# State-space stage of a streaming encoder step: turn counts rounded inside one PSUM sum, selection rows kept as constants over 16 partitions, and the sample's input columns transposed for 16 groups at once

## The chip, the cores and the metric

The program runs on one core of a Trainium2 chip. The metric is the device time of one launch, in microseconds. The core has a matrix engine (PE in the profile, its weight loads PEld), a vector engine (DVE), an activation engine (ACT), a general engine (POOL), and a queue engine (SP) that issues most of the transfers. Each engine takes its own instructions strictly in order, and semaphores hold an instruction until what it needs is there.

## The reference

One step of a two-layer encoder trunk. Layer 0 mixes tokens with a diagonal complex state-space layer and a gated product, layer 1 with sparse attention; a convolutional feed-forward block follows each. The prompt has 1,024 tokens, the sample 32 tokens with a state carried in. Only the state-space mixer matters here:

```python
def s5_mixer(u, h0_re, h0_im, lam_re, lam_im, log_dt, b_re, b_im, c_re, c_im, d_skip, w_glu, b_glu):
    uf = u.reshape(b, t, SSM_GROUPS, SSM_GROUP)               # 64 groups of 16 channels
    a_re, a_im, bb_re, bb_im = s5_discretize(...)             # a = exp(lambda*dt), 64 states a group
    bu_re = jnp.einsum('btgc,gpc->btgp', uf, bb_re)           # and bu_im
    bu_re = bu_re.at[:, 0].add(a_re * h0r - a_im * h0i)       # the carried state enters at token 0
    _, _, h_re, h_im = lax.associative_scan(_cplx_combine, (ar, ai, bu_re, bu_im), axis=1)
    y = einsum('btgp,gcp->btgc', h_re, c_re) - einsum('btgp,gcp->btgc', h_im, c_im)
    y = y + d_skip.reshape(SSM_GROUPS, SSM_GROUP) * uf
    z = jax.nn.gelu(y.reshape(b, t, D_MODEL))
    g = z @ w_glu + b_glu
    return g[..., :D_MODEL] * jax.nn.sigmoid(g[..., D_MODEL:]), h_re[:, -1], h_im[:, -1]
```

## The kernel before

**Blocks of 8 tokens.** The scan runs over blocks of 8 tokens: 128 blocks of the prompt and 4 of the sample, plus two columns that hold states, so a row has C = 134 columns. The 64 groups are taken as 8 output tiles `o` of 8 groups, and each tile as three sub-tiles `s` of 3, 3 and 2 groups (402, 402 and 268 columns).

**What is done for a sub-tile.** `angles(o, s)` computes, for every state and block, the rotation angle in turns, its cosine and sine, and the inputs laid out by block. `states(d, w)` multiplies inputs by the input maps, rotates, scans along the blocks on DVE (`en`) and rotates back (`pp`). `outputs(d, w)` sums three products into the output rows. For each tile, `taps(o)` builds the maps' factors (`ix`, `cp`) on DVE with helper products `tt` on POOL, and `maps(o, d)` forms `kr` and `inm` from them on PE and ACT.

**Order.** The code asks for `angles` two sub-tiles ahead of `states`, and for `taps` and `maps` of the next tile during the present one. A scheduler in the building layer merges this into one order for each engine. `angles` of a sub-tile stands on PE ahead of `states` two sub-tiles earlier, so everything that `angles` waits for on PE also holds that work.

**Angles.** A selection row `sel` is built on POOL for each sub-tile (L622): a constant row of block numbers `cval`, times the column of a 64-group identity, over 128 partitions. PE multiplies it with three weight tiles `wo` (high part, rounded part, low part of the turns per block). The first product (L626) goes to a PSUM tile of its own; DVE rounds it to whole turns by adding and subtracting a large constant (`kk`, L628); PE then sums the high part (L630), minus the whole turns (L631, weights `ngi`) and the low part (L632) in a second PSUM tile. ACT makes `cs` (cosine and sine) from that. Three prompt transposes (L641) and three sample transposes of 6 columns each (L642) fill one PSUM tile `pu`, which ACT copies to `ut` (L644).

**Sample inputs.** `ssm_input` normalizes the sample rows into `us` on DVE, moves them by 8 transfers from SBUF to SBUF into rooms that are free by then (L516), and copies them to 8 tiles `um` on ACT and DVE (L519, L521). It also makes the 8 prompt tiles `u` (L507), six on DVE and two on POOL.

**The scan's first column.** In `states`, ACT writes column 0 of `ga` from the carried state (L657). `ga` has two buffers, so this copy waits until the scan `en` two sub-tiles earlier has read its buffer. The next instructions on ACT wait behind it.

Of the kernel before, what the change touches and what calls it, by code (L numbers as in the profile page):

```python
# [41 lines left out]
MAGF = 12582912.0  # L42
# [8 lines left out]
class Trunk:  # L51
# [265 lines left out]
    def ssm_params(self, pool, tmp, ld):  # L317

        nc, I = self.nc, self.I
        G, N = 64, 64  # L320
# [112 lines left out]

        wo = pool.tile([P, 3, 2, N], F32R, name="wo")
        wof = wo.bitcast(F32)
        two = lambda v: v.rearrange("g (h n) -> g h n", h=1).to_broadcast([G, 2, N])
        nc.vector.tensor_copy(wo[:G, 1], two(pt))
        nc.scalar.mul(wo[G:, 1], two(pt), 0.0)
        nc.scalar.copy(wo[:G, 0], wof[:G, 1])
        nc.vector.tensor_sub(pt, pt, wof[:G, 1, 0])  # L440
        nc.vector.tensor_add(st, st, pt)
        nc.vector.tensor_copy(wo[:G, 2], two(st))
        nc.vector.tensor_scalar_add(t3, st, -2e-5)
        nc.scalar.copy(wo[G:, 0], two(t3))
# [36 lines left out]

    def ssm_input(self, tmp, ld):

# [27 lines left out]

        room = [v[0:6, i : i + 1024].rearrange("c (j f) -> c j f", f=P) for v in ld["free"] for i in range(0, 3072, 1024)]
        for o in range(KD):
            t = self.xp.tile([6, 8, 8, 16], F32, tag="xh", name="um", bufs=KD)
            r = room[o]
            nc.sync.dma_start(r, us[:, o * P : (o + 1) * P])  # L516
            v = r.rearrange("c j (g q) -> c g j q", q=16)
            if o in (2, 4, 6):
                nc.vector.tensor_copy(t, v)  # L519
            else:  # L520
                nc.scalar.copy(t, v)  # L521
            um.append(t)
        return u, um

    def ssm(self):

        nc, I, O = self.nc, self.I, self.O
        C = 134
        with ExitStack() as ctx:
            pool = ctx.enter_context(self.tc.tile_pool(name="ssm", bufs=1, reuse_waits="tile"))  # L530
            with self.tc.tile_pool(name="ssmt", bufs=1, reuse_waits="tile") as tmp:
                ld = self.ssm_loads(tmp)
                ngi = pool.tile([P, P], F32R, name="ngi")
                nc.vector.tensor_scalar_mul(ngi, self.ident, -1.0)
                swap = pool.tile([P, P], F32, name="swap")
                nc.sync.dma_start(swap, I["c_swap"])
                cval = pool.tile([P, C], F32, name="cval")
                nc.sync.dma_start(cval, I["c_cval"].to_broadcast([P, C]))
                id2 = pool.tile([P, 64], F32, name="id2")
                nc.vector.tensor_add(id2, self.ident[:, 0:64], self.ident[:, 64:128])  # L540
                fcs = pool.tile([P, 2, 2, 64], F32, name="fcs")
                tz = [pool.tile([P, 8, P], F32, name=f"tz{i}") for i in range(2)]
                m8s = [pool.tile([P, 8, C], F32, name=f"m8{i}") for i in range(2)]
                sels = [pool.tile([P, 3 * C], F32R, name=f"sel{i}") for i in range(3)]
                for t in tz:
                    nc.gpsimd.memset(t, 0.0)
                for t in m8s:
                    nc.gpsimd.memset(t[:, :, 0:6:5], 0.0)
                par = self.ssm_params(pool, tmp, ld)
                u, um = self.ssm_input(tmp, ld)  # L550
            smt, wo = par["smt"], par["wo"].rearrange("p v h n -> p v (h n)")
            mq = self._fill(pool, "mq", [P, 1], -0.25)
# [61 lines left out]
            def angles(o, s):  # L614

                g0 = G0[s]
                ng = min(3, 8 - g0)
                W, W2 = ng * C, W3(ng)
                v3 = lambda t: t[:, :W].rearrange("p (g c) -> p g c", c=C)
                gg = slice(8 * o + g0, 8 * o + g0 + ng)  # L620
                sel = sels[s]
                nc.gpsimd.tensor_mul(  # L622
                    v3(sel), cval.rearrange("p (g c) -> p g c", g=1).to_broadcast([P, ng, C]),
                    id2[:, gg].rearrange("p (g c) -> p g c", c=1).to_broadcast([P, ng, C]))
                pa = self.ps()
                nc.tensor.matmul(pa[:, :W2], wo[:, 0], sel[:, :W2], start=True, stop=True)  # L626
                kk = wk.tile([P, 3 * C], F32R, tag="kk", name="kk", bufs=1)
                nc.vector.tensor_scalar(kk[:, :W2], pa[:, :W2], MAGF, MAGF, op0=ALU.add, op1=ALU.subtract)  # L628
                pb = self.ps()
                nc.tensor.matmul(pb[:, :W2], wo[:, 1], sel[:, :W2], start=True, stop=False)  # L630
                nc.tensor.matmul(pb[:, :W2], ngi, kk[:, :W2], start=False, stop=False)  # L631
                nc.tensor.matmul(pb[:, :W2], wo[:, 2], sel[:, :W2], start=False, stop=True)  # L632
                cs = wk.tile([P, 2, 3, C], F32, tag="cs", name="cs", bufs=3)[:, :, :ng]
                cos, sin = cs[:, 0], cs[:, 1]
                nc.scalar.activation(cos, v3(pb), AF.Abs)
                nc.scalar.activation(sin, v3(pb), AF.Abs, bias=mq)
                nc.scalar.activation(cos, cos, AF.Sin, scale=-2 * math.pi, bias=self.halfpi)
                nc.scalar.activation(sin, sin, AF.Sin, scale=sc2, bias=bi2)
                pu = self.ps()
                for g in range(ng):  # L640
                    nc.tensor.transpose(pu[:, g * C + 6 : (g + 1) * C], u[o][:, g0 + g].rearrange("p j q -> p (j q)"), self.ident)  # L641
                    nc.tensor.transpose(pu[:, g * C : g * C + 6], um[o][:, g0 + g].rearrange("p j q -> p (j q)"), self.ident[:6, :6])  # L642
                ut = wk.tile([P, 3, C], F32, tag="ut", name="ut", bufs=3)[:, :ng]
                nc.scalar.copy(ut, v3(pu))  # L644
                return dict(o=o, s=s, g0=g0, ng=ng, gg=gg, v3=v3, cs=cs, cos=cos, sin=sin, ut=ut)

            def states(d, w):
# [138 lines left out]
    def glu(self, after_block):  # L786
# [3 lines left out]
        with self.tc.tile_pool(name="glu", bufs=2, reuse_waits="tile") as gp:  # L790
# [993 lines left out]
```

## Time and profile before

| what | value |
|---|---|
| time, median of 3 runs | 2750.98 us (2748.64 to 2754.19) |
| profiled execution: its own time | 2755.65 us |
| profiled execution: span of instructions | 2753.9 us |
| mean granted TensorE clock | 0.978 of full speed |
| PE busy over the span | 2576.4 us (94%) |
| DVE busy over the span | 1584.6 us (58%) |
| ACT busy over the span | 1006.8 us (37%) |
| POOL busy over the span | 434.5 us (16%) |

The state-space stage takes the first 262 us of the span. After it the gated product, the feed-forward blocks and the attention fill the rest. In the profile, a line such as L622 is a line of the kernel before; `out<-in` are the program's names. "Idle before" is the time in which an engine waited just ahead of an instruction, with the instruction that ended the wait.

### The profile page before, as it was taken

The numbers are of one execution on the slowest core, as the hardware profiler recorded it, in microseconds if no ns is written. First come the engines' busy times: TensorE is split into PE (matmuls) and PEld (weight loads), VectorE is DVE, ScalarE is ACT, GpSimd is POOL, SyncE is SP. The second block draws the span as 40 slices with busy tenths as digits, with TensorE's granted clock in tenths as the row PEclk, the third lists the DMA queues.
The fourth block names the chain that finished last, engine by engine and source line by source line (L and its number), as shares of the span: only waits on it lengthen the run. The fifth ranks groups of instructions, "written<-read, shape, count | busy, mean of one in ns | idle before, by whom it ended". The sixth has DMA issues, their size and how long they took to land. (4 is left out here: it accounts for less than half of the span.)

```text
span 2753.9 us, 43113 instructions
## 1 busy us (share of the span) xinstructions
PE 2576.4 (94%) x17203; PEld 2464.9 (90%) x17203; DVE 1584.6 (58%) x3300; ACT 1006.8 (37%) x2054; POOL 434.5 (16%) x659
## 2 busy tenths in 40 slices
PE   2888999999999999998898789999999999999999
PEld 2777999999999999997788667779999999999998
DVE  8885235544444444467799887663654444444443
ACT  4576223222222222234466667772322222222222
POOL 5553001100000000011245342220200000000000
PEclk9999999999999999998899899999999999999999
DMA  4234330111111111110111301203111111111111
GB/s 93 54 59 87 99 110 1 47 47 47 46 47 46 47 47 47 46 29 22 47 61 55 97 15 40 52 14 84 32 47 47 47 47 46 47 47 47 46 39 64
DMA packets 226253, 140.35 MB, mean 51 GB/s; under 512 B 50293, under 2 KB 218653, under 8 KB 226053
## 3 DMA queue, kind: packets, MB, share of 16 engines
q1 hardware_dynamic: 222309, 133.91, 17.8%
q8 instruction: 135, 2.21, 0.3%
q10 hardware_dynamic: 3104, 2.59, 0.3%
q0 software_dynamic: 640, 1.12, 0.2%
q14 instruction: 65, 0.53, 0.1%
HBM read 112.68 MB, written 13.40 MB: 46 GB/s over the span
## 5 line engine op out<-in xcount | busy, mean ns | idle before, releaser
L160 PE MATMUL ps_mm<-xh,whi 128*128 128x352 f32 x2304 | 746.7, 324 | 4.9 <-ACT whi L151 4.9
L162 PE MATMUL ps_mm<-xh,wlo 128*128 128x352 f32 x2304 | 746.0, 324 | 0.0
L161 PE MATMUL ps_mm<-xl,whi 128*128 128x352 f32 x2304 | 745.0, 323 | 0.0
L160 PEld LDWEIGHTS ps_mm<-xh,whi 128*128 128x128 f32 x2304 | 434.5, 189 | 5.1 <-ACT whi L151 5.1
L161 PEld LDWEIGHTS ps_mm<-xl,whi 128*128 128x128 f32 x2304 | 434.5, 189 | 0.0
L162 PEld LDWEIGHTS ps_mm<-xh,wlo 128*128 128x128 f32 x2304 | 434.3, 188 | 0.2 <-DVE wlo L152 0.2
L152 DVE TENSOR_TENSOR wlo<-wraw,whi 128x1024 fp32r<-128x1024 f32 (+1 forms) x145 | 175.4, 1221 | 419.0 <-ACT whi L151 419.0
L151 ACT CAST whi<-wraw 128x1024 fp32r<-128x1024 f32 (+1 forms) x145 | 149.7, 1046 | 715.1 <-PE ps_mm L161 696.7
L1656 DVE TENSOR_TENSOR xt<-xt,ps_mm 128x352 f32<-128x352 f32 x528 | 269.5, 521 | 191.5 <-PE ps_mm L162 191.3
L160 PE MATMUL ps_mm<-hh,whi 128*128 128x352 f32 x1056 | 341.2, 323 | 1.5 <-DVE xt L1656 1.5
L161 PE MATMUL ps_mm<-hl,whi 128*128 128x352 f32 x1056 | 341.1, 323 | 0.0
L162 PE MATMUL ps_mm<-hh,wlo 128*128 128x352 f32 x1056 | 340.8, 323 | 0.0
L1637 POOL COPY tails<-a 128x2 f32<-128x2 f32 x44 | 39.6, 900 | 1235.6 <-ACT a L1626 1235.6
L160 PEld LDWEIGHTS ps_mm<-hh,whi 128*128 128x128 f32 x1056 | 198.5, 188 | 2.1 <-DVE xt L1656 2.1
L162 PEld LDWEIGHTS ps_mm<-hh,wlo 128*128 128x128 f32 x1056 | 198.5, 188 | 0.0
L161 PEld LDWEIGHTS ps_mm<-hl,whi 128*128 128x128 f32 x1056 | 198.4, 188 | 0.0
L840 PE MATMUL ps_mm<-whi,xh 128*128 128x256 f32 (+3 forms) x560 | 162.5, 291 | 20.8 <-ACT raw L1241 20.7
L1644 DVE TENSOR_TENSOR c<-c,ps_mm 128x352 f32<-128x352 f32 (+2 forms) x176 | 71.6, 428 | 162.5 <-PE ps_mm L162 116.0
L841 PE MATMUL ps_mm<-wlo,xh 128*128 128x256 f32 (+3 forms) x560 | 161.5, 289 | 0.0
L842 PE MATMUL ps_mm<-whi,xl 128*128 128x256 f32 (+3 forms) x560 | 161.1, 289 | 0.0
L1626 ACT COPY a<-ps_mm 128x352 f32<-128x352 f32 (+2 forms) x176 | 61.9, 378 | 246.4 <-PE ps_mm L162 246.3
L840 PEld LDWEIGHTS ps_mm<-whi,xh 128*128 128x128 f32 (+1 forms) x560 | 103.9, 186 | 24.6 <-ACT raw L1241 23.4
(425 smaller groups left out, 4537.7 us busy)
## 6 DMA issues: line engine op xcount, KB each, us to landing
wraw<-in_ffn_w_up_dram SPq DMA_DIRECT2D x88, 512.0 KB
wraw<-in_ffn_w_down_dram SPq DMA_DIRECT2D x44, 512.0 KB
wraw<-in_attn_w_in_dram SPq DMA_DIRECT2D x14, 512.0 KB
graw<-in_ssm_w_glu_dram SPq DMA_DIRECT2D x104, 64.0 KB
xcm<-in_x_prompt_dram SPq DMA_DIRECT2D x8, 512.0 KB
cps<-cp SPq DMA_DIRECT2D x16, 256.0 KB
xcol<-in_x_prompt_dram SPq DMA_DIRECT2D x8, 512.0 KB
qr<-qd SPq DMA_DIRECT2D x32, 128.0 KB
```

Of the source, the lines that this page charges most:

```text
L151: nc.scalar.copy(hi, raw)
L152: nc.vector.tensor_sub(lo, raw, hi.bitcast(F32))
L160: nc.tensor.matmul(ps, wh, xh, start=(i == 0), stop=False)
L161: nc.tensor.matmul(ps, wh, xl, start=False, stop=False)
L162: nc.tensor.matmul(ps, wl, xh, start=False, stop=(i == n - 1))
L840: self.nc.tensor.matmul(ps, xh, hi[:, c, a:b], start=(k == 0), stop=False)
L841: self.nc.tensor.matmul(ps, xh, lo[:, c, a:b], start=False, stop=False)
L842: self.nc.tensor.matmul(ps, xl, hi[:, c, a:b], start=False, stop=(k == KD - 1))
L1626: nc.scalar.copy(u["a"][:, co + 2 : co + 2 + n], ps[:, to - b * BLK : to - b * BLK + n])
L1637: nc.gpsimd.tensor_copy(tails[:, u["f"], 0:2], u["a"][:, TP : TP + 2])
L1644: nc.vector.tensor_mul(h, h, bv[:, to - b * BLK : to - b * BLK + n])
L1656: nc.vector.tensor_add(self.xt[:, m, blocks[b]], self.xt[:, m, blocks[b]], ps[:, :BLK])
```

## The change

Four edits, all in the state-space stage; in all later stages the order of instructions on every engine is the same as before.

1. The turns are rounded in PSUM. One PSUM tile takes five products in a row: plus the large constant (a row of ones times `big`), minus the high part, minus the constant, plus the rounded part, plus the low part. The PSUM tile of the first product, `kk` on DVE and `ngi` are gone.
2. `sel` is a constant from the host over 16 partitions, loaded once and cast once; the weights `wo` are cut into 8 tiles `wog` of 16 partitions by 16 small transfers on POOL's queue.
3. The sample's columns go through DRAM: one transfer out (`usd`), 24 transfers back into a tile of 96 partitions, four transposes and one ACT copy to `uT`. The 64 small transposes are gone; POOL copies 6 columns a group from `uT` into `ut`.
4. The copy of column 0 of `ga` stands on POOL, not on ACT.

```diff
-    def ssm_input(self, tmp, ld):
+    def ssm_input(self, tmp, ld, uT, wo):
...
-        room = [v[0:6, i : i + 1024].rearrange("c (j f) -> c j f", f=P) for v in ld["free"] for i in range(0, 3072, 1024)]
+        with self.tc.tile_pool(name="usd", bufs=1, space=bass.MemoryType.DRAM) as dp:
+            usd = dp.tile([n, D], F32, name="usd")
+            nc.sync.dma_start(usd, us)
+            um = tmp.tile([96, 4, 8, 16], F32, name="um")
+            v = usd.rearrange("(c j) (t g q) -> c t g j q", j=8, t=4, q=16)
+            for c in range(6):
+                for t in range(4):
+                    nc.sync.dma_start(um[16 * c : 16 * c + 16, t], v[c, t])
+        ps = self.ps("aux")
+        for t in range(4):
+            nc.tensor.transpose(ps[:, 96 * t : 96 * t + 96], um[:, t].rearrange("p j q -> p (j q)"), self.ident[:96, :96])
+        nc.scalar.copy(uT, ps[:, :384].rearrange("p (t c g) -> p t c g", c=6, g=16))
+
+        ws = []
         for o in range(KD):
-            t = self.xp.tile([6, 8, 8, 16], F32, tag="xh", name="um", bufs=KD)
-            r = room[o]
-            nc.sync.dma_start(r, us[:, o * P : (o + 1) * P])
...
+            t = self.xp.tile([16, 3, P], F32R, tag="xh", name="wog", bufs=KD)
+            for h in range(2):
+                nc.gpsimd.dma_start(t[8 * h : 8 * h + 8], wo[64 * h + 8 * o : 64 * h + 8 * o + 8])
+            ws.append(t)
+        return u, ws
...
+                sel = pool.tile([16, 3, 3 * C], F32R, name="sel")
+                sraw = tmp.tile([16, 3, 3 * C], F32, name="sraw")
+                nc.scalar.dma_start(sraw, I["c_sel"])
+                nc.scalar.copy(sel, sraw)
...
-                nc.gpsimd.tensor_mul(
-                    v3(sel), cval.rearrange("p (g c) -> p g c", g=1).to_broadcast([P, ng, C]),
-                    id2[:, gg].rearrange("p (g c) -> p g c", c=1).to_broadcast([P, ng, C]))
-                pa = self.ps()
-                nc.tensor.matmul(pa[:, :W2], wo[:, 0], sel[:, :W2], start=True, stop=True)
-                kk = wk.tile([P, 3 * C], F32R, tag="kk", name="kk", bufs=1)
-                nc.vector.tensor_scalar(kk[:, :W2], pa[:, :W2], MAGF, MAGF, op0=ALU.add, op1=ALU.subtract)
+                w, st = wo[o], sel[:, s, :W2]
+
                 pb = self.ps()
-                nc.tensor.matmul(pb[:, :W2], wo[:, 1], sel[:, :W2], start=True, stop=False)
-                nc.tensor.matmul(pb[:, :W2], ngi, kk[:, :W2], start=False, stop=False)
-                nc.tensor.matmul(pb[:, :W2], wo[:, 2], sel[:, :W2], start=False, stop=True)
+                nc.tensor.matmul(pb[:, :W2], big[0:1, 0], ones[0:1, :W2], start=True, stop=False)
+                nc.tensor.matmul(pb[:, :W2], w[:, 0], st, start=False, stop=False)
+                nc.tensor.matmul(pb[:, :W2], big[0:1, 1], ones[0:1, :W2], start=False, stop=False)
+                nc.tensor.matmul(pb[:, :W2], w[:, 1], st, start=False, stop=False)
+                nc.tensor.matmul(pb[:, :W2], w[:, 2], st, start=False, stop=True)
...
-                    nc.tensor.transpose(pu[:, g * C + 6 : (g + 1) * C], u[o][:, g0 + g].rearrange("p j q -> p (j q)"), self.ident)
-                    nc.tensor.transpose(pu[:, g * C : g * C + 6], um[o][:, g0 + g].rearrange("p j q -> p (j q)"), self.ident[:6, :6])
+                    nc.tensor.transpose(pu[:, g * P : (g + 1) * P], u[o][:, g0 + g].rearrange("p j q -> p (j q)"), self.ident)
                 ut = wk.tile([P, 3, C], F32, tag="ut", name="ut", bufs=3)[:, :ng]
-                nc.scalar.copy(ut, v3(pu))
+                a = o % 2 * 8 + g0
+                nc.gpsimd.tensor_copy(ut[:, :, 0:6], uT[:, o // 2, :, a : a + ng].rearrange("p c g -> p g c"))
+                nc.scalar.copy(ut[:, :, 6:], pu[:, : ng * P].rearrange("p (g c) -> p g c", c=P))
...
-                nc.scalar.copy(ga[:, :, 0], smt[:, 33, w["gg"]])
+                nc.gpsimd.tensor_copy(ga[:, :, 0], smt[:, 33, w["gg"]])
...
-            gp.tile([P, 2 * P + 64], F32, name="pad", bufs=1)
+            gp.tile([P, 2 * P - 24], F32, name="pad", bufs=1)
```

The first place is POOL at the start of the stage, from the first prompt tile `u` that POOL makes. Before, it reads (numbers tell tiles of one name apart):

```order
L507 TENSOR_TENSOR u_491<-xcm_97,rsx_443 128x8x8x16
L622 TENSOR_TENSOR sel0_128<-cval_119,id2_121 128x402
L622 TENSOR_TENSOR sel1_129<-cval_119,id2_121 128x402
L622 TENSOR_TENSOR sel2_130<-cval_119,id2_121 128x268
L507 TENSOR_TENSOR u_497<-xcm_103,rsx_443 128x8x8x16
L569 TENSOR_TENSOR tt_538<-smt_279,bsw_352 128x1024
L593 TENSOR_TENSOR dgi_554<-ident_61,dg_439 16x128
```

Now 16 transfers stand there in place of three `sel` products, 13 of them between the second `u` and the first `tt`:

```order
L507 TENSOR_TENSOR u_490<-xcm_97,rsx_442 128x8x8x16
L529 DMA wog_538<-wo_336 8x384 x2
L529 DMA wog_541<-wo_336 8x384
L507 TENSOR_TENSOR u_496<-xcm_103,rsx_442 128x8x8x16
L529 DMA wog_541<-wo_336 8x384
L529 DMA wog_544<-wo_336 8x384 x2
L529 DMA wog_547<-wo_336 8x384 x2
L529 DMA wog_550<-wo_336 8x384 x2
L529 DMA wog_553<-wo_336 8x384 x2
L529 DMA wog_556<-wo_336 8x384 x2
L529 DMA wog_559<-wo_336 8x384 x2
L581 TENSOR_TENSOR tt_575<-smt_278,bsw_351 128x1024
```

Behind the last row come `dgi`, three copies to `ut`, two copies to `ga`, two clears of `pp`, and only then the second `tt` of the tile.

The second place is PE in the middle of the stage, `angles` of a sub-tile of two groups (L608 belongs to `maps`, L653 and L654 to `states`). Before:

```order
L626 MATMUL ps_mm<-sel_130,wo 128x268
L630 MATMUL ps_mm<-sel_130,wo 128x268
L641 MATMUL ps_mm<-ident,u 128x128
L642 MATMUL ps_mm<-ident,um 128x6
L641 MATMUL ps_mm<-ident,u 128x128
L608 MATMUL ps_aux<-ident,ix 128x128 x4
L631 MATMUL ps_mm<-kk,ngi 128x268
L632 MATMUL ps_mm<-sel_130,wo 128x268
L642 MATMUL ps_mm<-ident,um 128x6
L653 MATMUL ps_mm<-ut,inm 128x134 x2
```

Now the five products of the sum stand together, and no product of the group waits for DVE:

```order
L636 MATMUL ps_mm<-ones,big 128x268
L637 MATMUL ps_mm<-sel,wog 128x268
L638 MATMUL ps_mm<-ones,big 128x268
L639 MATMUL ps_mm<-sel,wog 128x268
L640 MATMUL ps_mm<-sel,wog 128x268
L649 MATMUL ps_mm<-ident,u 128x128 x2
L662 MATMUL ps_mm<-ut,inm 128x134 x2
```

The third place is ACT where the copies of `kr` stand that `maps` of the next tile needs. Before, a copy to `ga` stands ahead of them:

```order
L637 ACTIVATE cs<-cs,halfpi 128x402
L638 ACTIVATE cs<-cs,bi_531,sc_530 128x402
L657 COPY ga<-smt 128x3
L600 COPY kr<-ps_aux 16x512 x2
L644 COPY ut<-ps_mm 128x402
```

Now it is gone, and `kr` follows the sine at once:

```order
L645 ACTIVATE cs<-cs,halfpi 128x402
L646 ACTIVATE cs<-cs,bi_566,sc_565 128x402
L612 COPY kr<-ps_aux 16x512 x2
L653 COPY ut<-ps_mm 128x3x128
L693 COPY yo<-ps_mm 128x402
```

## Rows read from the trace of the kernel before

**Rows 1.** Busy time of each engine in two stretches, granted clock at the end.

```profile
149.00:176.00 27.00, 22.18 (x130) 18.68 (x128) 20.64 (x25) 19.10 (x38) 12.55 (x15) 0.81 0.30 57
123.00:223.00 100.00, 83.86 (x529) 70.78 (x528) 79.55 (x93) 69.71 (x139) 53.91 (x68) 0.88 0.34 65
```

The columns are the stretch, its length, busy us (instructions) of PE, PEld, DVE, ACT and POOL, PE's clock, the DMA share and GB/s.

**Rows 2.** Timeline of DVE: first rotation of tile 0 and of tile 7.

```profile
81.67 0.56 DVE L659 TENSOR_TENSOR ga<-ps_mm,cs 128x399 f32<-128x399 f32 x1
...
243.39 0.57 DVE L659 TENSOR_TENSOR ga<-ps_mm,cs 128x399 f32<-128x399 f32 x1 [0.25 <-PE ps_mm L653]
```

The columns are start, duration, engine, line and operation; in brackets the idle time before and what ended it.

**Rows 3.** Timeline of PE: first products and transposes of one `angles` call.

```profile
101.55 0.43 PE L626 MATMUL ps_mm<-sel,wo 128*128 128x402 f32 x1
101.81 0.34 PE L630 MATMUL ps_mm<-sel,wo 128*128 128x402 f32 x1
102.00 0.27 PE L641 MATMUL ps_mm<-ident,u 128*128 128x128 f32 x1
102.20 0.22 PE L642 MATMUL ps_mm<-ident,um 6*128 6x6 f32 x1
102.35 0.33 PE L641 MATMUL ps_mm<-ident,u 128*128 128x128 f32 x1
```

**Rows 4.** Waits of PE in 76 to 262 us: total, times, longest.

```profile
PE ps_aux L608 <- ACT kr L600: 9.3, 5, 4.1
...
PE ps_mm L631 <- DVE kk L628: 3.2, 5, 1.3
```

**Rows 5.** Timeline of DVE, ACT and PE around two waits for `kr`.

```profile
159.21 2.63 DVE L663 TENSOR_TENSOR_SCAN en<-m,ga 128x402 f32<-128x402 f32 x1
...
161.88 0.20 ACT L657 COPY ga<-smt 128x3 f32<-128x3 f32 x1 [3.13 <-DVE en L663]
161.88 1.00 DVE L667 TENSOR_TENSOR pp<-en,cs 128x804 f32<-128x804 f32 x1
162.19 1.05 ACT L600 COPY kr<-ps_aux 16x512 f32<-16x512 f32 x2
...
162.82 1.97 PE L608 MATMUL ps_aux<-ident,ix 128*128 128x128 f32 x8 [4.07 <-ACT kr L600]
...
211.63 1.13 PE L608 MATMUL ps_aux<-ident,ix 128*128 128x128 f32 x8 [3.29 <-ACT kr L600]
```

**Rows 6.** Groups by line and shape, 55 to 262 us: the wide rounding.

```profile
L628 DVE TENSOR_SCALAR kk<-ps_mm 128x402 fp32r<-128x402 f32 x16 | 9.0, 565 | 2.6 <-PE ps_mm L626 2.6
```

The columns are busy us, mean ns of one, and the idle time before them.

**Rows 7.** Timeline of the start, and of eight transfers on POOL's queue.

```profile
44.50 9.39 POOL L507 TENSOR_TENSOR u<-xcm,rsx 128x1024 f32<-128x1024 f32 x1 [4.00 <-DVE rsx L174]
...
45.36 2.64 SPq L516 DMA_DIRECT2D bb<-us  x3
...
48.07 1.04 ACT L521 COPY um<-bb 6x1024 f32<-6x1024 f32 x1 [4.07 <-DMA bb<-us]
...
52.06 2.37 DVE L519 COPY um<-bb 6x1024 f32<-6x1024 f32 x1
...
58.38 2.02 POOL L569 TENSOR_TENSOR tt<-smt,bsw 128x1024 f32<-128x1024 f32 x1
...
62.61 1.20 DVE L576 TENSOR_TENSOR cp<-smt,ca 128x1024 f32<-128x1024 f32 x1
...
68.92 1.86 DVE L577 TENSOR_TENSOR cp<-cp,tt 128x1024 f32<-128x1024 f32 x1 [2.35 <-POOL tt L574]
...
75.59 5.14 SPq L603 DMA_DIRECT2D tz<-kr  x8
...
213.07 4.36 POOL L748 DMA_DIRECT2D g<-in_ssm_w_glu_dram  x8
```

**Rows 8.** Timeline of POOL: multiplier rows and copies of 8 and 12 elements.

```profile
219.39 1.75 POOL L583 TENSOR_SCALAR m<-smt 128x32 f32<-128x32 f32 x2 [1.96 <-DVE en L663]
221.09 0.19 POOL L669 COPY fcs<-pp 128x8 f32<-128x8 f32 x1
...
228.10 1.13 POOL L669 COPY fcs<-pp 128x12 f32<-128x12 f32 x1 [2.28 <-DVE pp L667]
```

More of the change, by code (lines that the diff above doesn't have):

```diff
@@ L432, in ssm_params @@
         nc.vector.scalar_tensor_tensor(st, raf, kb, st, op0=ALU.mult, op1=ALU.add)
-        wo = pool.tile([P, 3, 2, N], F32R, name="wo")
+        wo = tmp.tile([P, 3, 2, N], F32R, name="wo")
         wof = wo.bitcast(F32)
@@ L438, in ssm_params @@
         nc.scalar.mul(wo[G:, 1], two(pt), 0.0)
-        nc.scalar.copy(wo[:G, 0], wof[:G, 1])
+        nc.scalar.mul(wo[:G, 0], wof[:G, 1], -1.0)
         nc.vector.tensor_sub(pt, pt, wof[:G, 1, 0])
@@ L532, in ssm @@
                 ld = self.ssm_loads(tmp)
-                ngi = pool.tile([P, P], F32R, name="ngi")
-                nc.vector.tensor_scalar_mul(ngi, self.ident, -1.0)
+                big = pool.tile([16, 2, P], F32R, name="big")
+                for i, v in enumerate((MAGF, -MAGF)):
+                    nc.vector.tensor_scalar(big[:, i], self.ident[:16], 0.0, v, op0=ALU.mult, op1=ALU.add)
                 swap = pool.tile([P, P], F32, name="swap")
                 nc.sync.dma_start(swap, I["c_swap"])
[L537 to L540, printed above, removed]
                 fcs = pool.tile([P, 2, 2, 64], F32, name="fcs")
@@ L543, in ssm @@
                 m8s = [pool.tile([P, 8, C], F32, name=f"m8{i}") for i in range(2)]
-                sels = [pool.tile([P, 3 * C], F32R, name=f"sel{i}") for i in range(3)]
+                sel = pool.tile([16, 3, 3 * C], F32R, name="sel")
+                sraw = tmp.tile([16, 3, 3 * C], F32, name="sraw")
+                nc.scalar.dma_start(sraw, I["c_sel"])
+                nc.scalar.copy(sel, sraw)
+                uT = pool.tile([P, 4, 6, 16], F32, name="uT")
                 for t in tz:
@@ L549, in ssm @@
                 par = self.ssm_params(pool, tmp, ld)
-                u, um = self.ssm_input(tmp, ld)
-            smt, wo = par["smt"], par["wo"].rearrange("p v h n -> p v (h n)")
+                u, wo = self.ssm_input(tmp, ld, uT, par["wo"].rearrange("p v h n -> p v (h n)"))
+            smt = par["smt"]
             mq = self._fill(pool, "mq", [P, 1], -0.25)
@@ L557, in ssm @@
             wk = ctx.enter_context(self.tc.tile_pool(name="ssmw", bufs=1, reuse_waits="tile"))
+            ones = wk.tile([16, 3 * C], F32R, tag="kk", name="ones", bufs=1)
+            nc.vector.tensor_scalar(ones, self.ident[:16, 0:1].to_broadcast([16, 3 * C]), 0.0, 1.0, op0=ALU.mult, op1=ALU.add)
             G0 = (0, 3, 6)
@@ L1734, in host_constants @@
     ident = np.eye(P, dtype=f)
-    cval = np.concatenate([np.arange(5), [0], np.arange(128)]).astype(f)[None]
+    cval = np.concatenate([np.arange(5), [0], np.arange(128)]).astype(f)
+    sel = np.zeros((2, 8, 3, 3, 134), f)
+    for g in range(8):
+        sel[:, g, g // 3, g % 3] = cval
     inv = np.array([0x3F800000, 0x3E4693AF, 0x3D1A08C8, 0x3BEEF74E, 0x3AB95D22, 0x398FC8F8, 0x385F10C4, 0x372D07A7], np.uint32).view(f)
@@ L1745, in host_constants @@
         "c_swap": np.roll(ident, 64, axis=0),
-        "c_cval": cval,
+        "c_sel": sel.reshape(16, 3, 402),
     }
```

10 lines of the change are left out of this document (1 added, 9 removed).

## The prediction

> **What bounds the kernel now.** I read the page's busy times first: PE is busy for 94% of the span. All later stages hang on PE and keep their order, so a shift at the end of the state-space stage (262 us) should arrive at the end of the run unchanged. Only that stage is left to price. Next I read the windows in it. From 123 to 223 us PE is busy for 83.9 of 100 us and DVE for 79.6; PE's granted clock is 0.88, and in 149 to 176 us it is 0.81 [rows 1]. So PE is not full here, and its clock drops. The timeline of DVE gives the period of a tile: the first rotation of tile 0 starts at 81.67, that of tile 7 at 243.39 us [rows 2], 161.7 us for seven tiles, 23.1 us each. DVE's share of that is 0.796 x 23.1 = 18.4 us. The stage is thus bound neither by PE nor by DVE alone but by a loop of waits between engines; the list of PE's waits names the links. The largest are `kr` from ACT (9.3 us in 5 waits, longest 4.1) and `kk` from DVE (3.2 us in 5) [rows 4].
>
> The last look is at the start, where everything up to tile 0 is a chain of its own [rows 7].
>
> **Part one: the steady tiles.**
>
> *PE rows.* Per sub-tile group one 6x6 transpose goes. Its step to the next row is 0.15 us (102.20 to 102.35) [rows 3]; 56 of the 64 lie in tiles 1 to 7, so 8.4 us. The wide products: before, the first of a run takes a step of 0.26 us and the next 0.19 [rows 3], and the four stood in two runs, so 2 x 0.45 = 0.90 us. Now five stand in one run: 0.26 + 4 x 0.19 = 1.02. That costs 0.12 x 21 sub-tiles = 2.5 us. I assume that a product over 16 or 1 rows of the contraction takes as long as one over 128, since its step is set by its columns; no row shows it for these. Net 6 us less on PE.
>
> *The round trip for the turns.* `kk` goes, and with it 3.2 us of PE's waits [rows 4] and 565 ns of DVE each for 16 wide ones [rows 6], with the narrow ones about 1.34 us of DVE for a tile. A PSUM tile per sub-tile is also freed.
>
> *The `ga` copy ahead of `kr`.* This is the clearest cause in the trace. At 161.88 ACT begins the `ga` copy after 3.13 us without work, when `en` ends; `kr` follows at 162.19, and PE, which waited 4.07 us, goes on at 162.82 [rows 5]. Without the copy `kr` could start when ACT ran dry, at 158.75, 3.4 us earlier. PE's clock was at 0.81 in the stretch around it [rows 1]: over 27 us that is 27 x 0.19 = 5.1 us of full-speed work lost, part of which a PE without this hole keeps. But PE does not gain all: DVE's `pp` still ends at 162.88 [rows 5], and the outputs need it. I take 6 us for this wait with its clock, 5 us for the one of 3.29 us at 211.63 [rows 5], and 1 us for the rest, 12 in all.
>
> The sum of these is 6 + 3 + 12 = 21 us for seven tiles. I give a third of it back. DVE's own work, 18.4 − 1.3 = 17.0 us a tile, is a floor at 7 x 6.1 = 43 us of gain and does not forbid it; but when the `kr` wait goes, `pp` and `cp` of DVE are late next, and they don't move with this edit. So **−14 us**. Bounds: −30 if the clock also stays up through the stretch of 0.81 and the waits behind `pp` go with it; +3 if every gain is taken by the next wait and the PE rows cost their 2.5.
>
> *What POOL takes over.* The copies to `ut` and `ga` are small. A POOL copy of 8 elements a partition took 0.19 us, one of 12 that came while DVE worked 1.13 us [rows 8]. Two for each sub-tile are 6 x 0.2 to 6 x 1.1 = 1.2 to 6.8 us of POOL a tile, where it is busy for 54 of 100 us [rows 1]: there is room. I cost them at nothing. Their cover is the distance to `states` two sub-tiles on; if that goes, rival four comes true.
>
> [...]
>
> **Part two: the start.** Two chains meet at `maps` of tile 0.
>
> *POOL's chain.* POOL's first `u` is held from 44.50 to 53.89 while DVE makes its six, and came through when DVE's `um` copy began (52.06) [rows 7]. That copy is gone: DVE goes straight on to two products of 1.20 us (`ix`, `cp`), so I let `u` end at about 57. Then 3 transfers at 4.36/8 = 0.545 us [rows 7] to 58.6, the second `u` (as `tt`, the same shape, 2.0) to 60.6, 13 transfers (7.1) to 67.7, and `tt` (2.02) to 69.7; before, `tt` ended at 60.40 [rows 7]. DVE then adds (1.2) and multiplies (1.2); POOL's eight small rows (0.2 each) end at about 73.6, the second `tt` at 75.6, and the addition to `cp` at 76.8. Before, it ended at 70.78 [rows 7]: 6 us later. Some of that comes back, because the taps of tile 1, which before were spread between these, now follow each other. I put the first rotation of tile 0 at 85.5 in place of 81.67: **+4 us**.
>
> *SP's chain.* The transfer out starts at 45.36 and lands after about 2.7 us (the three before it were issued at 45.36, and ACT's copy began at 48.07 when the first was there [rows 7]), so by 48 to 49.5. 24 transfers at 5.14/8 = 0.64 us [rows 7] are 15.4 us, to 64 or 65; with a landing at 66 to 67 the transposes, the copy to `uT` and three `angles` calls stand before `states`. At the lower clock these are 8 to 9 us: about 75, just under POOL's chain. PE takes the four transposes in order, so its first `angles` waits for the last of the 24 transfers; before, PE's first products waited for `sel` instead.
>
> Bounds for the start: 0 if POOL gets its `u` in two or three us earlier and tile 1's taps absorb the rest; +9 if the 24 transfers take 0.72 to 0.88 us each (1.9 to 5.8 us more) and everything behind them moves.
>
> Before the change no row shows a POOL transfer while DVE is busy. [...]
>
> **The sum.** −14 + 4 = −10 us. Against the profiled run's own 2755.65 us this is 2745.6; that run stands 4.67 us above the median of the three (2750.98), so the median should be **2741 us**, a change of −0.36%. About 0.2% (5.5 us) is what a measurement of this kernel can tell from no change.
>
> **The rivals.**
>
> *One, the next wait takes it.* When `kr` comes early, `pp` and `cp` set the period, and only the 6 us of PE rows count. For it: DVE at 79.6% and every link behind it on DVE. Against it: at 161.88 the wait hung on the copy, not on `pp`. −6 + 4 = −2: **2749**, no change to be told.
>
> *Two, POOL's transfers at the start are held by DVE.* 16 transfers at up to 1.13 instead of 0.545 us are 16 x 0.58 = 9 us; but DVE has only about 5 us of ready work there before it needs `tt` itself, so +5: start +9, net −5, **2746**, also within 0.2%. The mechanism is that of POOL's `u` at 44.50 [rows 7].
>
> *Three, everything is given.* All 21 us of the steady part, and PE's clock stays up where it read 0.81 (another 5.1 us): −26 + 2 = −24, **2727**. For it: the holes of 3 to 4 us stand just where the clock is low. Against it: the waits for `pp` stay.
>
> *Four, slower: POOL becomes late.* The copies to `ut` and `ga` now stand in POOL's order between the multiplier rows `m` and `fcs`, which wait for `en` and `pp` of DVE [rows 8]. A sub-tile has 23.1 / 3 = 7.7 us; the scan itself takes 2.63 [rows 5], so 5.1 us lie between the end of one and the start of the next, for which `ga` must be there. POOL needs 1.75 us for `m` and, if `fcs` and both copies are held as at 228.10, 3 x 1.13 more: 5.1 us. That is the point from which it decides: one more held row makes each of 21 scans 1.13 us late, 23.7 us. The 21 us of part one are off it, the start's 4 on it: +7, so the median is **2758**. Against it: POOL idles for 46% of that stretch [rows 1], and its copies of 8 elements came through in 0.19.
>
> **How the numbers follow.** Chances: forecast 0.45, rival one 0.20, two 0.08, three 0.12, four 0.15. Faster by over 0.2%: forecast and three, 0.57. Within: one and two, 0.28. Slower: 0.15. The range takes one and two wholly, the nearer half of three, and the nearer half of four: 2728 to 2757. The forecast's own range, faster cases alone, is 2734 to 2745.
>
> **What would show it.** Right: no wait of PE for `kk`; `kr` on ACT with no idle time behind `en`; granted clock above 0.81 around the fourth tile; a period of about 21 us (23.1 − 14/7); the first rotation of tile 0 at 84 to 87 us. Wrong: POOL copies of over 0.5 us in most sub-tiles with PE waiting for `ut` (rival four); transfers on POOL's queue of over 0.8 us each (two); a period above 22.3 with waits for `pp` and `cp` grown (one). What would upset the whole: a stage-end shift that later stages swallow, or a wide product over 16 rows whose step is not 0.19 us.

## The result, and the profile after

The changed kernel takes 2734.84 us (median of 4 runs, 2732.57 to 2738.98) against 2751.02 us before (4 runs): a ratio of 0.994, 95% interval 0.9929 to 0.9952, or 16.2 us less. Forecast were 2741 us, a range of 2728 to 2757, and faster as the likeliest case. The profiled execution took 2738.98 us (span 2737.2), 16.7 us less than that of before.

The two stretches of [rows 1], after the change (same columns):

```profile
123.00:223.00 100.00, 88.49 (x632) 76.34 (x633) 83.65 (x101) 82.04 (x152) 63.25 (x98) 0.97 0.41 79
149.00:176.00 27.00, 23.25 (x174) 19.99 (x173) 24.50 (x29) 21.38 (x42) 17.65 (x21) 1.00 0.39 68
```

PE is busier in the same 100 us and its granted clock is 0.97, not 0.88; in the stretch that read 0.81 it is 1.00. (The same times hold other work now; over the seven tiles the clock is 0.95, and 0.91 before.) DVE's timeline gives the period, as [rows 2] did:

```profile
85.78 0.56 DVE L668 TENSOR_TENSOR ga<-ps_mm,cs 128x399 f32<-128x399 f32 x1
...
223.66 0.57 DVE L668 TENSOR_TENSOR ga<-ps_mm,cs 128x399 f32<-128x399 f32 x1 [0.25 <-PE ps_mm L662]
```

The first rotation comes 4.1 us later than before, that of tile 7 comes 19.7 us earlier: seven tiles take 137.9 us in place of 161.7, so 23.8 us are gained and 4.1 lost. Of these 19.7, 16.7 reach the end. PE's granted clock in 240 to 260 and 260 to 300 us was 1.00 twice before and is 0.91 and 0.96 now; 20 x 0.09 + 40 x 0.04 = 3.4 us, about the 3.0 that are missing. That the clock is the cause is not shown: in a second profile of the changed kernel (below) tile 7 comes 18.1 us earlier than before and the end 21.6, so what follows tile 7 differs by 6.5 us between two profiles of one kernel.

PE's waits from 76 to 262 us, in answer to [rows 4]:

```profile
PE ps_mm L691 <- DVE pp L676: 4.5, 3, 3.9
PE ps_aux L611 <- DVE cp L589: 4.1, 4, 1.9
...
PE ps_aux L131 <- DMA vrow<-in_ffn_conv_w_dram: 2.3, 1, 2.3
...
PE ps_mm L690 <- DVE ix L583: 1.6, 1, 1.6
...
PE ps_mm L691 <- POOL ga L666: 1.2, 1, 1.2
...
PE ps_aux L620 <- ACT kr L612: 0.5, 1, 0.5
```

The 9.3 us for `kr` are 0.5, the 3.2 for `kk` are gone, and the waits for `pp` and `cp`, 5.4 and 4.5 before, did not grow. Other waits did. PE now reaches the transposes of `vrow` (constants of this and later stages) at 131 us, not at 137, and stands there for 2.3 us until a transfer lands. From the first rotation of tile 0 to that of tile 7 all the waits that this view lists for PE come to 17.6 us, against 22.9 before: 5.3 less, not 12. The price on POOL is there, in the groups of POOL's instructions of the same stretch (busy us, mean ns, idle time before):

```profile
L666 POOL COPY ga<-smt 128x3 f32<-128x3 f32 x14 | 10.3, 733 | 13.0 <-DVE en L672 13.0
...
L666 POOL COPY ga<-smt 128x2 f32<-128x2 f32 x8 | 7.7, 968 | 3.0 <-DVE en L672 2.9
L652 POOL COPY ut<-uT 128x12 f32<-128x12 f32 x7 | 6.5, 931 | 10.9 <-PE ps_mm L690 10.9
...
L652 POOL COPY ut<-uT 128x18 f32<-128x18 f32 x14 | 5.3, 379 | 2.4 <-PE ps_mm L690 2.4
```

These copies took 0.4 to 1.0 us on average, not 0.2; but PE waited for them once, 1.2 us.

### The profile page after: what moved, and what is told of

Same layout as the page of the kernel before. It is cut to its first block, busy times and chain, and to the rows that moved or that the text cites. A ratio compares the mean times of both kernels' runs of the same rounds, so it can differ in the third digit from the quotient of the medians.

```text
span 2737.2 us, 43112 instructions
## 1 busy us (share of the span) xinstructions
PE 2566.2 (94%) x17167; PEld 2459.5 (90%) x17167; DVE 1560.4 (57%) x3275; ACT 1001.9 (37%) x2027; POOL 442.0 (16%) x699
## 4 chain that ended last, share of the span: by engine, by line
PE 77%; DVE 13%; ACT 4%; issue 3%; DMA 1%; POOL 1%; SPq 1%; ACTq 0%; DVEq 0%; POOLq 0%
PE ps_mm L162 19%; PE ps_mm L160 19%; PE ps_mm L161 19%; DVE junk L1169 4%; PE ps_o L1425 2%; PE ps_mm L793 2%; PE ps_mm L792 2%; PE ps_mm L791 2%; PE ps_t L1435 2%; PE ps_s L1399 1%; PE ps_s L1400 1%; ACT p L1409 1%; DVE p L1401 1%; DVE small L1182 1%; DVE score L1031 0%
```

## The experiments

"Steady" is the time from the first rotation of tile 0 to that of tile 7, from one profile each: 161.7 us before, 137.9 after. Ratios are to the kernel before on the same chip; intervals are of 95%.

**One edit alone, and one undone.** The `ga` copy moved to POOL in the kernel before:

```diff
-                nc.scalar.copy(ga[:, :, 0], smt[:, 33, w["gg"]])
+                nc.gpsimd.tensor_copy(ga[:, :, 0], smt[:, 33, w["gg"]])
```

> The kernel before with one edit: the copy of column 0 of ga stands on POOL, not on ACT. Theory L (the late kr behind that copy was the main loss): 12 us less than before, 2739 us, and PE's wait for kr falls from 9.3 us to under 2. Theory R (the gain comes from PE's rows and from the round trip for the turns; the next wait takes what the copy held): within 3 us of before, 2748 to 2751. POOL late (rival four of the prediction): slower than before.

2743.26 us, ratio 0.9965 (0.9951 to 0.9979), 9 us less; steady 153.0 us. The waits of PE say where the rest went:

```profile
PE ps_mm L631 <- DVE kk L628: 12.1, 10, 3.2
...
PE ps_aux L608 <- ACT kr L600: 1.1, 2, 0.6
```

The wait for `kr` fell from 9.3 to 1.1 us as theory L said, but `kk` rose from 3.2 to 12.1: the next wait on the same in-order engine took all of it. What gained the 9 us stands in the windows from the first rotation of tile 0 to that of tile 7, of the kernel before and of this run (columns as in [rows 1]):

```profile
81.67:243.39 161.72, 140.27 (x907) 118.52 (x907) 131.84 (x160) 108.40 (x215) 82.14 (x104) 0.91 0.33 64
```

```profile
81.89:234.90 153.01, 133.07 (x907) 111.75 (x907) 131.46 (x161) 106.04 (x195) 94.45 (x125) 0.96 0.34 68
```

PE runs the same number of rows, 907, and is busy for 7.2 us less, at a granted clock of 0.96 in place of 0.91; its idle time falls by only 1.5 us, from 21.5 to 19.9. The clock alone accounts for that: 140.27 x 0.91/0.96 = 133.0. So most of this edit's gain came as PE's clock. The opposite, the same line put back on ACT in the changed kernel:

> The changed kernel with the copy of column 0 of ga back on ACT. Theory L: the 12 us come back, 2747 us, with a wait of PE for kr of 6 to 9 us in total. Theory R: within 3 us of the changed kernel's 2735.

2754.15 us, 1.001 (1.0001 to 1.0019): 19 us slower than the changed kernel (17 against its second measurement, below) and not faster than the kernel before. Steady 153.1. Both theories were too low: the other three edits without this one bring nothing at the end of the run, though tile 7 still comes 4.7 us earlier than before. (In both runs the scheduler lets a few neighbours change places with the line.) The mechanism stands in ACT's and PE's timelines of this run:

```profile
205.97 0.20 ACT L666 COPY ga<-smt 128x3 f32<-128x3 f32 x1 [5.37 <-DVE en L672]
206.34 1.05 ACT L612 COPY kr<-ps_aux 16x512 f32<-16x512 f32 x2 [0.17 <-DMA cps<-cp]
...
206.97 1.97 PE L620 MATMUL ps_aux<-ident,ix 128*128 128x128 f32 x8 [3.31 <-ACT kr L612]
```

ACT stands 5.37 us before a copy of three elements, `kr` behind it, and PE behind `kr`; the eight transposes then take 1.97 us where the same eight took 1.13 at 160.20 in this run; PE's granted clock is 0.74 from 200 to 220 us. This is [rows 5] over again. It is not the whole loss: PE's wait for `kr` is 7.9 us in this run, that for `pp` 10.0 in place of 4.5, and over the seven tiles PE's busy time is 7.9 us longer than in the changed kernel (128.02 and 120.17 us for 853 rows each) and its idle time 7.4 us.

**The rounding alone.** In the kernel before, five products as in the diff, with `sel` still over 128 partitions:

> The kernel before with one edit: turns rounded by five products in PSUM, with the selection rows still built on POOL over 128 partitions. Theory L: 1 to 4 us less, 2747 to 2750, since 3 us of waits and 1.3 us of DVE a tile go but PE gets 2.5 us more. Theory R: 8 us less or more, 2743 or under, because DVE's relief shortens the loop. If the extra product matters more than the wait: 2752 to 2754.

2759.89 us, 1.0026 (1.0015 to 1.0036): 7.5 us slower, steady 170.2 us. Neither theory had this. PE's timeline of that run, one run of products:

```profile
230.34 0.44 PE L629 MATMUL ps_mm<-ones,big 1*128 1x402 f32 x1
230.72 0.45 PE L630 MATMUL ps_mm<-sel,wo 128*128 128x402 f32 x1
231.09 0.45 PE L631 MATMUL ps_mm<-ones,big 1*128 1x402 f32 x1
231.47 0.45 PE L632 MATMUL ps_mm<-sel,wo 128*128 128x402 f32 x1
231.76 0.35 PE L633 MATMUL ps_mm<-sel,wo 128*128 128x402 f32 x1
231.95 0.27 PE L642 MATMUL ps_mm<-ident,u 128*128 128x128 f32 x1
```

The step, from start to start, is 0.37 to 0.38 us around the products with weights of 1 row, 0.29 from the fourth to the fifth and 0.19 from there to the next row, where all have 128 rows. The granted clock is 1.00 from 228 to 233 us, so it is not the clock. A new theory (S): such a change of row count costs PE about 0.19 us. To test it, the same products with weights of 128 rows throughout:

```diff
-                big = pool.tile([16, 2, P], F32R, name="big")
-                for i, v in enumerate((MAGF, -MAGF)):
+                big = pool.tile([P, 2, P], F32R, name="big")
+                for i, v in enumerate((MAGF / P, -MAGF / P)):
...
-                nc.tensor.matmul(pb[:, :W2], big[0:1, 0], ones[0:1, :W2], start=True, stop=False)
+                nc.tensor.matmul(pb[:, :W2], big[:, 0], ones[:, :W2], start=True, stop=False)
```

> The kernel before with the rounding in PSUM alone, as in the run of that name, but the row of ones and its weights stand over 128 partitions (each weight 1/128 of the constant), so that all five products have the same number of rows. Theory S (a product costs more when the number of rows of its weights changes from the product before it: 0.38 us a step in place of 0.19): four changes in each of 24 runs go, 4 x 24 x 0.19 = 18 us less than the 2760 of that run, 2742. Rival (the run of five products itself, or what it pushes back, costs the 8 us): 2757 to 2760.

2747.06 us, 0.9985 (0.9976 to 0.9994): 12.8 us less than with one row, 5 us less than before; steady 157.1. The steps are 0.18 to 0.19 behind the first, which is 0.27:

```profile
171.48 0.43 PE L629 MATMUL ps_mm<-ones,big 128*128 128x402 f32 x1
171.75 0.34 PE L630 MATMUL ps_mm<-sel,wo 128*128 128x402 f32 x1
171.93 0.34 PE L631 MATMUL ps_mm<-ones,big 128*128 128x402 f32 x1
172.11 0.35 PE L632 MATMUL ps_mm<-sel,wo 128*128 128x402 f32 x1
```

So S holds, with 13 of its 18 us; the order of instructions on PE is the same in both runs. Over the seven tiles PE's busy time fell by 21.2 us (155.70 to 134.54) and its idle time grew by 8.0. Why PE pays for such a change is not shown by these runs, only what it pays: steps of 0.37 to 0.38 us in place of 0.18 to 0.19 for 402 columns. In the changed kernel the products stand over 1 and 16 rows and the steps between them are 0.18 to 0.19 us behind the first, so this cost isn't paid between 1 and 16 rows:

```profile
177.75 0.45 PE L636 MATMUL ps_mm<-ones,big 1*128 1x402 f32 x1
178.04 0.34 PE L637 MATMUL ps_mm<-sel,wog 16*128 16x402 f32 x1
178.23 0.34 PE L638 MATMUL ps_mm<-ones,big 1*128 1x402 f32 x1
178.42 0.34 PE L639 MATMUL ps_mm<-sel,wog 16*128 16x402 f32 x1
178.60 0.34 PE L640 MATMUL ps_mm<-sel,wog 16*128 16x402 f32 x1
178.87 0.55 PE L649 MATMUL ps_mm<-ident,u 128*128 128x128 f32 x3
179.25 0.39 PE L662 MATMUL ps_mm<-ut,inm 128*128 128x134 f32 x2
```

Edit 2 is thus what makes edit 1 cheap here; rows of ones over 128 partitions are another way. The reverse in the changed kernel, rounding on DVE again (`kk`, `ngi` over 128 rows between products over 16):

```diff
-                nc.tensor.matmul(pb[:, :W2], big[0:1, 0], ones[0:1, :W2], start=True, stop=False)
+                nc.tensor.matmul(pa[:, :W2], w[:, 0], st, start=True, stop=True)
+                kk = wk.tile([P, 3 * C], F32R, tag="kk", name="kk", bufs=1)
+                nc.vector.tensor_scalar(kk[:, :W2], pa[:, :W2], MAGF, MAGF, op0=ALU.add, op1=ALU.subtract)
+                nc.tensor.matmul(pb[:, :W2], w[:, 1], st, start=True, stop=False)
+                nc.tensor.matmul(pb[:, :W2], ngi, kk[:, :W2], start=False, stop=False)
```

> The changed kernel with the turns rounded on DVE again (kk, ngi over 128 partitions; selection rows and weights stay over 16). By the prediction's terms: 3 us of waits and 1.3 us of DVE a tile come back, 2.5 us of PE go: 2736 to 2740. Theory S adds two changes of row count in each run, 2 x 24 x 0.19 = 9 us: 2744 to 2750.

2745.65 us, 0.9977 (0.9967 to 0.9986), 8 to 11 us slower than the changed kernel; steady 150.4. As S said, and the steps between weights of 128 and of 16 rows are 0.39 and 0.37 us (at 179.10 and 179.49 in this run, granted clock 1.00). But the wait for `kk` is 10.2 us in 10 waits here, so both causes share the loss, and this run doesn't part them.

**The small transposes.** One 6x6 transpose more for each group in the changed kernel, into columns that are not read:

```diff
                     nc.tensor.transpose(pu[:, g * P : (g + 1) * P], u[o][:, g0 + g].rearrange("p j q -> p (j q)"), self.ident)
+                    nc.tensor.transpose(pu[:, 3 * P + 6 * g : 3 * P + 6 * g + 6], u[o][:6, g0 + g].rearrange("p j q -> p (j q)"), self.ident[:6, :6])
```

> The changed kernel with one 6x6 transpose more for each group (64 in all), into columns of the PSUM tile that nobody reads; it prices the 64 transposes that the change took away. If PE's rows count fully, as the prediction's first term says: 64 x 0.15 = 9.6 us more than 2735, 2744. If PE's free time covers them: under 3 us more.

2741.4 us, 0.9968 (0.9955 to 0.998), 4 to 7 us over the changed kernel's two medians; steady 148.4, 9 to 10.5 us more, in a profile whose run took 2747.01 us, 5.6 above the median. PE pays more than the prediction's 0.15 us:

```profile
186.24 0.22 PE L650 MATMUL ps_mm<-ident,u 6*128 6x6 f32 x1
186.39 0.33 PE L649 MATMUL ps_mm<-ident,u 128*128 128x128 f32 x1
186.65 0.22 PE L650 MATMUL ps_mm<-ident,u 6*128 6x6 f32 x1
186.81 0.33 PE L649 MATMUL ps_mm<-ident,u 128*128 128x128 f32 x1
```

A pair takes 0.41 to 0.42 us (186.24 to 186.65). Without the small one, three transposes take 0.38 us (178.87 to 179.25), 0.13 each. A 6x6 transpose costs 0.28 us of PE, half of it as the slower step of its neighbour: by theory S, 6 rows beside 128. Not all of it becomes time: over the seven tiles PE's busy time is 21.7 us longer than in the changed kernel, and its idle time 11.2 us shorter.

**Two edits together.** The kernel before with the `ga` copy on POOL and the rounding over 128 rows:

> The kernel before with two edits: the copy of column 0 of ga on POOL, and the rounding in PSUM with all products over 128 partitions. Alone they gave 9 and 5 us. If gains add: 2738. If one in-order wait hides the other (with the ga copy gone, PE's wait for kk grew from 3.2 to 12.1 us; with kk gone, the wait for kr stayed at 8.9): more than the sum, 2728 to 2734.

2732.77 us, 0.9931 (0.9917 to 0.9944): 20 us less than before where the parts alone give 9 and 5; steady 146.7, 15.0 less, where the parts give 8.7 and 4.7; no wait for `kr` or `kk` among PE's larger ones. That the wait for `kr` had hidden the one for `kk` is shown by the run with the `ga` copy alone, where `kk` rose; that the pair gives more than the sum is not clear of the noise of three measurements. These two edits, without edits 2 and 3, do as well as the whole change within the noise: the start is 4.6 us earlier and the steady tiles are 8.9 us longer.

**POOL's small copies.** The copy of 6 columns to `ut` on ACT:

```diff
-                nc.gpsimd.tensor_copy(ut[:, :, 0:6], uT[:, o // 2, :, a : a + ng].rearrange("p c g -> p g c"))
+                nc.scalar.copy(ut[:, :, 0:6], uT[:, o // 2, :, a : a + ng].rearrange("p c g -> p g c"))
```

> The changed kernel with the small copies to ut on ACT, not on POOL. If POOL's held copies cost anything in the steady tiles: 2 to 5 us less, 2730 to 2733. If they are covered and ACT has room: within 2 us of 2735. If a small copy ahead of kr on ACT delays kr again: 2738 to 2745.

2741.26 us, 0.9959 (0.9945 to 0.9972); steady 138.7. The interval overlaps that of the changed kernel, so no difference can be told; there is no gain, and POOL's held copies are not what limits the tiles. The time lies in the third theory's range, but its sign is missing: PE's wait for `kr` is not in the list of this run.

**The start.** The changed kernel was run again beside the last three:

> The changed kernel once more, unchanged, as the measure for the others of this call: 2733 to 2739 us by the four runs known; every theory expects the same here.

2737.59 us, 0.9945 (0.9932 to 0.9959); steady 139.5 us, so this measure moves by 1.6 us between two profiles of one kernel. The weights' transfers on ACT's queue in place of POOL's:

```diff
-                nc.gpsimd.dma_start(t[8 * h : 8 * h + 8], wo[64 * h + 8 * o : 64 * h + 8 * o + 8])
+                nc.scalar.dma_start(t.bitcast(F32)[8 * h : 8 * h + 8], wo.bitcast(F32)[64 * h + 8 * o : 64 * h + 8 * o + 8])
```

> The changed kernel with the 16 small transfers of the weights issued on ACT's queue, not on POOL's. Theory (POOL's chain sets the start): 16 x 0.52 = 8.4 us go from it, PE's three angles calls end at 67.6 and become the bound, so the first rotation comes 6 to 7 us earlier, at 79, and the time is 2728 to 2729. Rival (SP's 24 transfers set it, or DVE's taps): first rotation within 2 us of 85.8, time 2733 to 2735.

2738.39 us, 0.9955 (0.9943 to 0.9968), first rotation at 85.97: nothing gained, as the rival had it for the rotation. POOL was freed (`tt` ready at 59.94, not 68.29), but ACT's and SP's queues show another bound:

```profile
47.38 22.62 SPq L519 DMA_DIRECT2D um<-usd  x24
...
56.14 10.19 ACTq L529 DMA_DIRECT2D wog<-wo  x14
```

SP's 24 transfers took 22.62 us, where they take 11.20 in the changed kernel; PE's first transposes moved from 58.55 to 70.04. The gain on POOL's chain was lost on SP's. So POOL's chain was tested without touching a queue, by giving DVE all eight `u`:

```diff
-            (nc.gpsimd if o % 3 == 2 else nc.vector).tensor_mul(
+            nc.vector.tensor_mul(
```

> The changed kernel with all eight prompt tiles u made on DVE; POOL makes none at the start. Theory (POOL's first u, held for 11.9 us while DVE works, and the queue of transfers behind it set the start): POOL's first tt is ready 10 us or more earlier, PE's angles calls that end at 67.6 become the bound, the first rotation comes at 78 to 80 us in place of 85.8 and the time is 2728 to 2730. Rival (the transfers of the sample's columns on SP, or the taps, set it anyway): first rotation within 2 us of 85.8. Rival (POOL's 16 transfers are held in turn while DVE makes the tiles): their time grows beyond 0.8 us each and the first rotation stays after 82.

2722.25 us, 0.9886 (0.9873 to 0.99), 15 us below the changed kernel on that chip, and the fastest of all. The changed kernel's POOL against this run's:

```profile
44.07 11.94 POOL L507 TENSOR_TENSOR u<-xcm,rsx 128x1024 f32<-128x1024 f32 x1 [2.70 <-DVE rsx L174]
55.95 1.76 POOL L529 DMA_DIRECT2D wog<-wo  x3
57.73 1.91 POOL L507 TENSOR_TENSOR u<-xcm,rsx 128x1024 f32<-128x1024 f32 x1
59.57 6.67 POOL L529 DMA_DIRECT2D wog<-wo  x13
66.26 2.03 POOL L581 TENSOR_TENSOR tt<-smt,bsw 128x1024 f32<-128x1024 f32 x1
```

```profile
46.41 3.29 POOL L529 DMA_DIRECT2D wog<-wo  x6 [4.84 <-DVE u L507]
49.93 4.43 POOL L529 DMA_DIRECT2D wog<-wo  x8 [0.23 <-DVE u L507]
54.71 1.03 POOL L529 DMA_DIRECT2D wog<-wo  x2 [0.34 <-issue]
55.75 2.93 POOL L581 TENSOR_TENSOR tt<-smt,bsw 128x1024 f32<-128x1024 f32 x1
```

The first product `u` held POOL for 11.94 us with all the transfers queued behind it. Without it they go out while DVE works, at 0.55 us each, not held, and `tt` is done at 58.68, 9.6 us earlier. PE's last transposes of the three `angles` calls now run straight into `maps`, at 67.93, and the first rotation comes at 74.42, 11.4 us earlier where 6 to 8 were expected: a delay that I had left out goes too. In the changed kernel `ix` on DVE, just ahead of the first rotation, takes 3.40 us (82.46 to 85.86) beside a `tt` on POOL from 82.76; here that `tt` starts behind `ix`, which takes 1.35. At tile 7 the lead over the second profile of the changed kernel is 10.4 us, and 11.5 us at the end of these two profiles. So in these runs products of DVE and POOL that ran side by side could take far longer (`u` on POOL 11.94 us, and 1.91 with DVE idle; `ix` on DVE 3.40, and 1.35 ahead of `tt`), while POOL's transfers beside DVE's products took 0.55 us each, against 0.51 with DVE idle: rival two of the prediction, in which they are held, is not seen. Why the products took longer is not shown. Last, on top of that, the sample's columns by 6 transfers out and 6 back:

```diff
-            nc.sync.dma_start(usd, us)
+            for c in range(6):
+                nc.sync.dma_start(usd[c].rearrange("g j q -> j g q"), us[8 * c : 8 * c + 8].rearrange("j (g q) -> j g q", q=16))
...
-                for t in range(4):
-                    nc.sync.dma_start(um[16 * c : 16 * c + 16, t], v[c, t])
+                nc.sync.dma_start(um[16 * c : 16 * c + 16], usd[c].rearrange("(t g) j q -> g t j q", t=4))
```

> The run with all u on DVE, and the sample's columns by 6 transfers out and 6 back in place of 1 and 24. Theory (each small transfer costs SP about 0.47 us, and PE's first angles wait for the last): the four transposes start 4 us earlier, at 54 to 55 in place of 58.5, the first rotation at 75 to 76, the time 2724 to 2726. Rival (the longer write, in pieces of 64 bytes, takes what the shorter queue gives): no change against the run before, 2728 to 2730.

2725.75 us, 0.9902 (0.9889 to 0.9916): no gain over the run before, though the time and the rotation (76.17) are about what the theory named. PE's transposes start at 54.00 as expected, but PE then waits 2.69 us for `cp` until 65.19, and `ix` on DVE, beside POOL's `tt` again, takes 3.41 us just ahead of the first rotation. With the queue shortened, POOL's and DVE's chain of the taps is the bound; the rival's reason (64-byte pieces) was not the one: the transposes that need the last piece start 4.6 us earlier.

## Why the prediction came out, point by point

**The start, +4.** Right in its sum (+4.1 us, first rotation at 85.78 where 85.5 stood) and in its cause: POOL's chain was the later one, as PE's waits in the changed kernel show.

```profile
58.55 1.59 PE L522 MATMUL ps_aux<-ident,um 96*128 96x96 f32 x4 [16.86 <-DMA um<-usd]
...
74.80 3.57 PE L611 MATMUL ps_aux<-cp,ix 128*16 128x128 f32 x16 [7.02 <-DVE cp L589]
```

Its parts were off in both directions, and that the sum came out to 0.3 us is luck. SP's transfers took 11.20/24 = 0.47 us each, not 0.64, so that chain lay 7 us under POOL's, not just under it. On POOL the held `u` took 11.94 us to 56.0 (57 said), the 13 transfers 0.51 each, `tt` ended at 68.29 (69.7 said) and the addition to `cp` at 74.65 (76.8 said). The 2.2 us so won were lost again: from there to the first rotation it took 11.1 us, as before (10.9), not 8.7, with `ix` of 3.40 us at the end. Rival two was not put to the test in the changed kernel, where DVE had no work while the transfers went; in the run with all `u` on DVE they went beside DVE's products at 0.55 us each, where the prediction named over 0.8 as the rival's sign, so no run shows a transfer held by DVE. From the first of the four transposes to the end of the three `angles` calls PE took 9.2 us (58.55 to 67.78; 8 to 9 said). Its wide products stepped by 0.33 us there and by 0.18 to 0.19 from 82 us on, but the granted clock reads 1.00 in 58 to 68 us as in 81 to 86: no row shows the prediction's "lower clock" there as a granted clock, and the cause of the slower steps is not shown.

**The steady tiles, −14.** The direction was right, the size was not: 23.8 us. Two terms were off. "I give a third of it back" was to stand for `pp` and `cp` being late next, and their waits stayed at 4.5 and 4.1 us; what came back of the 12 us of `kr` and `kk` were other waits, `vrow` first. And the rows of PE were priced too low. The undiscounted sum was 21. Of its terms:

- PE rows, −6 net: the 6x6 transposes were priced at their own step of 0.15 us and cost 0.28 with that of the next row, so 56 are 15.7 us of PE, not 8.4. Five products take 1.12 us (177.75 to 178.87), not 1.02, since the step from 16 rows back to 128 is 0.27; the narrow ones take 0.82 (102.17 to 102.99) in place of 0.68 before. By these steps PE has some 11.5 us less to do in seven tiles, an estimate. In time the transposes are worth less: put back, all 64 cost 4 to 7 us. That five products cost so little more held only because edit 2 makes them 1 and 16 rows; my assumption that a product's step is set by its columns alone was wrong for 1 beside 128 (0.38 us for 402 columns, where products over 128 rows in a row stepped by 0.18 to 0.19).
- `kk`, −3: 5 us alone (rounding over 128 rows), and 8 to 11 when it is undone in the changed kernel, with the changes of row count that come back with it. Its relief of DVE was added up too low, 1.34 us a tile: the narrow one takes 0.43, so 2 x 0.565 + 0.43 = 1.56.
- `ga`, −12: 9 us alone and 17 to 19 when it is the last edit. It is the largest term, as said, but terms don't add in a loop of in-order waits.

**What was said to show it.** No wait for `kk`, `kr` straight behind the sine, clock at 1.00 around the fourth tile: all seen. ACT around the place of [rows 5], after the change:

```profile
156.38 0.72 ACT L646 ACTIVATE cs<-cs,bi,sc 128x402 f32<-128x402 f32 x1
157.00 1.04 ACT L612 COPY kr<-ps_aux 16x512 f32<-16x512 f32 x2
```

The period is 137.9/7 = 19.7 us, not 21. What POOL takes over was held much as in rival four's condition (0.4 to 1.0 us a copy), yet the 5.1 us of room sufficed: one wait of 1.2 us. Whether later stages swallow some of the shift can't be told: 3 of 19.7 us are missing in one profile, and in the other the end gained 3.5 us more than tile 7.

Where PE's rows are the same, its busy and idle time part the clock from the waits: most of what `ga` alone gave was clock, and put back as the last edit it cost about as much in busy as in idle time. For the whole change the rows differ too, and how the 23.8 us divide between fewer rows, clock and waits stays open.

## What to carry to other kernels

An instruction that waits on an in-order engine costs what stands behind it, and taking it away shows its worth only when the next wait of the same loop goes too (the `ga` copy: 9 us alone, 17 to 19 as the last edit): try edits in pairs and as the last one removed. Price a matmul with the row ahead of it: in these runs weights of 1, 6 or 16 rows among weights of 128 cost about two steps for one (402 columns: 0.38 us with 1 row and 0.37 to 0.39 with 16, against 0.19; a 6x6 transpose 0.28 with its neighbour's slower step, against 0.13 for one of 128), so keep small ones together. At a start-up chain, look for a long instruction that is held at the head of a queue of transfers (11.94 us here); moving those two products of POOL was worth 15 us, nearly as much as the whole change with its 16.2.

## What the hardware showed that I had not expected

- A change between weights of 1 and of 128 rows took PE's step from 0.19 to 0.38 us for 402 columns, at a granted clock of 1.00; between 1 and 16 rows it stayed at 0.18 to 0.19.
- One copy of three elements moved to another engine left PE's waits at the same total (12.5 us for `kr` and `kk` before, 13.2 after) and raised its granted clock from 0.91 to 0.96, which gave 7.2 of 8.7 us.
- 24 small transfers on SP's queue took 11.2 us beside 16 on POOL's queue (all `u` on DVE), and 22.6 us beside 16 on ACT's.
- Transfers on POOL's queue took 0.55 us each while DVE made `u` (all `u` on DVE); in the changed kernel a product on POOL took 11.94 us beside the same work of DVE, and the next one 1.91 with DVE idle.
